# Score products on all 128 array rows in a two-layer hybrid trunk

## The chip, the core and the metric

The kernel runs on one core of a Trainium2 chip. A core has five engines with queues of their own: TensorE (matrix products; PE in the profile, its weight loads PEld), VectorE (DVE), ScalarE (ACT), GpSimd (POOL) and SyncE (SP), which issues the transfers here. The metric is the device time of one execution in microseconds (us); less is better. The time of the kernel before is the median of three runs, 1939.88 us (1935.67 to 1942.19).

## The reference

A trunk of two layers works on 512 latent tokens and 256 context tokens of width 1024, all in float32. Each layer takes a modulated RMS norm, projects it into four groups of heads, joins what the groups return, projects back, and adds; then a gated MLP of width 2816 with a short convolution does the same. The groups are:

- A: four query heads of 64 features on two key heads, with normalised and rotated q and k, softmax over all 768 keys;
- B: a state-space scan in both directions;
- C: as A, but over a window of 128 latent keys to either side and all context keys, with an extra sink logit;
- D: latent attention, four heads whose q and k have 64 features from a low-rank product and 32 rotated ones, 96 together.

Scores are a product over the head's features, 64 in A and C and 96 in D:

```python
s = jnp.einsum('bqkgd,bnkd->bkgqn', q, k).astype(jnp.float32) * scale
p = jax.nn.softmax(s, axis=-1)
return jnp.einsum('bkgqn,bnkd->bqkgd', p.astype(v.dtype), v)
```

Context tokens are queries too in the first layer, and read context keys only; in the second layer there are latent queries alone.

## The kernel before

Features lie on the partitions and tokens along the columns. To keep float32 accuracy, each operand of a product is held as a high part and a low part (`split`, lines 136 to 138: ScalarE rounds the high part, VectorE subtracts; `psplit`, lines 140 to 142, subtracts on GpSimd), and a product is the sum of high x high, low x high and high x low. Every product is issued by `mm` (line 134), so all of TensorE's products carry that line in the profile, and the names of the tiles tell them apart: psi are projections, pss scores, pspt the transposes of the probabilities, psy the values, psq and psk the up-projections of latent attention.

Grouped attention (A and C, `gqa`, line 617) puts a trick on the 128 rows. A query head has 64 features, so one tile `qh` holds the high part of q in one half of its rows (`rh`) and the low part in the other (`rl`; `get_q`, lines 645 to 649). The tile `kh` has the high part of k in both halves, and `kl` the low part in both (`get_kv`, lines 626 to 633; GpSimd writes `kl`). The first product, `qh` with `kh` over 128 rows, sums high x high and low x high at once. The second, line 668, is cut to the 64 rows `rh` and gives high x low. Each of the two is issued for at most 512 columns of keys at a time: a block of 128 queries over 768 keys takes 512 + 256 columns, C's blocks over 640 or 512 keys take 512 + 128 or 512, context queries take 256. C adds its window's mask by a 128-column bf16 product (`cb`).

Latent attention (D, `mla_prologue`, line 1107) has 64 + 32 features in one tile, so it has separate tiles `dqh`, `dql`, `dkh`, `dkl` and three products of 96 rows each (line 1183). `get_pair` (line 1147) makes the tiles of two heads: it projects q (psq), writes rows 0 to 63 by `split`, rows 64 to 95 from the rotated part, projects k (psk) and does the same; the low part of k's rotated rows is subtracted on GpSimd (`psplit`, dkl). Rows 96 to 127 of these tiles aren't written.

A block's way is the same in all three groups (`attention`, line 585): the scores go to one of two PSUM buffers of two banks; VectorE takes the maximum (nm, line 524), ScalarE the exponential with its sum (p, line 531), VectorE the reciprocal, GpSimd scales p (line 538); three blocks later TensorE transposes p, ScalarE and VectorE split it, and TensorE forms the values. Tiles of heads are prepared up to ten blocks ahead (`AHEAD`).

`run` (line 144) traces several streams side by side by weights: A's attention beside C's projections, C's attention beside the projections of D and B, and the scan of B beside the modulation of later stages and latent attention (lines 1217, 1218, 1233). A scheduler of the language then orders the instructions of each engine by these priorities and assigns buffers (41 of the kind `s3`, 16 of `w4`); each engine works off its own queue in order.

Of the kernel before, what the change touches and what calls it, by code (L numbers as in the profile page):

```python
# [17 lines left out]
D = 1024  # L18
SEQ = 512
CTX = 256  # L20
TOK = SEQ + CTX
# [67 lines left out]
def trunk(ctx: ExitStack, tc: tile.TileContext, a, out):  # L89
# [54 lines left out]
    def run(*streams):  # L144
        """Traces streams side by side, each advanced in proportion to its weight."""
        live = [[g, w, 0.0] for g, w in streams]
        while live:
            s = min(live, key=lambda e: e[2])
            try:
                next(s[0])  # L150
                s[2] += 1.0 / s[1]
            except StopIteration:
                live.remove(s)
# [8 lines left out]

# [1 line left out]
    x = []  # L164
# [24 lines left out]

# [1 line left out]
    cact = P1.tile([128, KD, 32], F32, tag="cact", name="cact")  # L191
# [24 lines left out]
    def mod_pool(l, chs):  # L216
        """The same by Pool, features on partitions; the tensor engine sums the partitions."""
        for hc in [2 * ch + c for ch in chs for c in range(2)]:
            accs = s3("macc", F32, (2, 256))
            for q in range(2):  # L220
                wm = w4("wm", (4, 256), F32)
                nc.sync.dma_start(wm, a["wmod"][l, hc, q])
                for g in range(4):
                    first = q == 0 and g == 0
                    tmp = accs if first else s3("mtmp", F32, (2, 256))
                    for t in range(2):
                        pool.tensor_scalar(tmp[:, t], wm[:, g], cact[:, 4 * q + g, t:t + 1], 1.0, op0=ALU.mult, op1=ALU.mult)  # L227
                    if not first:
                        pool.tensor_tensor(accs, accs, tmp, op=ALU.add)
                    yield  # L230
            ps = b1("psm")
            for t in range(2):
                for i in range(2):
                    mm(ps[:, 2 * t + i:2 * t + i + 1], accs[:, t, 128 * i:128 * i + 128], ones[:, 0:1], True, True)
            dve.tensor_tensor(
                mod[l][:, :, 2 * hc:2 * hc + 2], ps[:, 0:4].rearrange("p (t i) -> p t i", i=2),
                par_at(l, "bmod", 2 * hc, 2).unsqueeze(1).to_broadcast([128, 2, 2]), op=ALU.add)
            yield
# [7 lines left out]

# [1 line left out]
    def rstd_steps(ps, n, w, y):  # L248
        v, t = tiny("nv", w), tiny("nt", w)
        dve.tensor_scalar(v, ps[:, :w], 1.0 / n, EPS, op0=ALU.mult, op1=ALU.add)  # L250
        yield
        # a first guess from the exponent's half, then Newton's steps
        dve.tensor_scalar(t.bitcast(I32), v.bitcast(I32), 1, None, op0=ALU.logical_shift_right)
        yield
        dve.tensor_scalar(y.bitcast(I32), t.bitcast(I32), -1.0, float(0x5F3759DF), op0=ALU.mult, op1=ALU.add)
        yield
        for _ in range(3):
            dve.scalar_tensor_tensor(t, y, -0.5, v, op0=ALU.mult, op1=ALU.mult)
            yield
            dve.tensor_tensor(t, t, y, op=ALU.mult)  # L260
            yield
            dve.scalar_tensor_tensor(y, t, 1.5, y, op0=ALU.add, op1=ALU.mult)
            yield
# [7 lines left out]
    def bcast(cols, segs, tiles, heads=1):  # L271
        """PSUM [128, tokens] whose column t is cols[t] (per group of 128 / heads partitions)."""
        for s, ps in zip(segs, tiles):
# [17 lines left out]
    class Norm:  # L291
        """RMS norm of the residual stream, part by part of the tokens; scaled, shifted and split for products."""

# [87 lines left out]
    def first_item(norm, tiles, halfway=None):  # L381
        """The first products after a norm, each of them advanced as the norm's features come."""
        def load():
# [4 lines left out]
        def begin(hls):  # L388
# [6 lines left out]
            def quanta():  # L395
                cuts = (0, KD) if halfway else (0, KD)
                seen = set()
                for k0, k1 in zip(cuts, cuts[1:]):
                    for i, (sl, s) in enumerate(norm.parts):
# [5 lines left out]
                        for k in range(k0, k1):  # L405
                            norm.step(i, k)
                            for n, (hl, (segs, _), pl, pc) in enumerate(zip(hls, tiles, lat, ctx or lat)):
                                if s not in segs:
                                    continue
                                p = pc if s else pl[:, sl]  # L410
                                # the first two products of the context share a bank
                                for j, (wi, hh) in enumerate(((0, norm.hi), (0, norm.lo), (1, norm.hi))):
# [27 lines left out]
    def gemm(items):  # L440
        """Items are (load, begin): begin(load()) gives the quanta of a product and what follows it; the
        steps that follow are traced beside the next products. The next item is loaded with an item's first
        quantum, or a later one."""
        posts = []
# [35 lines left out]

    # ================= token mixers =================
    def mixers(l, norm, halfway, mods):
# [19 lines left out]

# [1 line left out]
        class Half:  # L504
            """256 queries of a head: two blocks of latent queries, or the context's queries."""

# [110 lines left out]
        def gqa(q, k, vt, sinkp, banded, ys):  # L617
            # the banded group keeps its keys in the order lat0 lat1 ctx0 ctx1 lat2 lat3
            kmap = [(0, 256, 0), (512, 256, 256), (256, 256, 512)] if banded else [(0, TOK, 0)]
# [3 lines left out]
            for kv in range(2):  # L623
# [16 lines left out]
                for hh in range(2):  # L640
# [18 lines left out]

                    def sc_mm(ps, q0, c0, w, masks=(), get_kv=get_kv, get_q=get_q, rh=rh):  # L660
                        kh, kl = get_kv()[:2]
                        qh = get_q()
                        qs = slice(q0, q0 + 128)
                        for o in range(0, w, 512):
                            n = min(512, w - o)
                            mm(ps[:, o:o + n], qh[:, qs], kh[:, c0 + o:c0 + o + n], True, False)
                            ms = [m for m in masks if o <= m[1] < o + n]
                            mm(ps[:, o:o + n], qh[rh, qs], kl[rh, c0 + o:c0 + o + n], False, not ms)
                            for i, (mi, mo) in enumerate(ms):
                                mm(ps[:, mo:mo + 128], cb[:, 0, :], cb[:, mi, :], False, i == len(ms) - 1)  # L670
# [38 lines left out]

# [1 line left out]
        qn = tiny("qn", 1)  # L711
# [35 lines left out]

        # V of A and C and dt of B: tokens on partitions
        def v_item(j, box=[]):
# [31 lines left out]

# [1 line left out]
        def c_post(sc, segs, box):  # L783
# [18 lines left out]

# [1 line left out]
        dq, dkv, d_low = [], [], []  # L804
# [53 lines left out]

# [1 line left out]
        zs, xbc = [], []  # L860
# [47 lines left out]

# [1 line left out]
        y_b = []  # L910
# [13 lines left out]
        def scan():  # L924
# [10 lines left out]
            for n in (15, 13, 11, 9, 7, 5, 3):  # L935
# [7 lines left out]
                                     op0=ALU.mult, op1=ALU.mult)  # L943
            # per (direction, chunk, head): running sums, decay of a chunk, weights of its state
            cs, tot, wd, dec, dtd = (tiny(n) for n in ("cs", "tot", "wd", "dec", "dtd"))
# [155 lines left out]

# [1 line left out]
        y_d = []  # L1103
# [3 lines left out]
        def mla_prologue():  # L1107
# [36 lines left out]
            yield  # L1144
            halves = mla_halves
            for pr in range(2):
                def get_pair(pr=pr):
                    qps = up_q(pr)
                    r = []
                    for hh in range(2):  # L1150
                        hd = 2 * pr + hh
                        rh = slice(64 * hh, 64 * hh + 64)
                        qh_, ql_ = s3("dqh", F32R), s3("dql", F32R)
                        for s, p in zip(qsegs, qps):
                            split(qh_[0:64, SEG[s]], ql_[0:64, SEG[s]], p[rh])
# [8 lines left out]
                    for hh in range(2):  # L1164
                        rh = slice(64 * hh, 64 * hh + 64)
                        kh_, kl_ = s3("dkh", F32R), s3("dkl", F32R)
                        for s, p in zip(both, kps):
                            split(kh_[0:64, SEG[s]], kl_[0:64, SEG[s]], p[rh])
# [6 lines left out]
                for hh in range(2):  # L1175
                    hd = 2 * pr + hh

                    def sc_mm(ps, q0, segs, get_pair=get_pair, hh=hh):
                        qh_, ql_, kh_, kl_ = get_pair()[0][hh]
                        qs = slice(q0, q0 + 128)  # L1180
                        for jj, (q_, k_) in enumerate(((qh_, kh_), (ql_, kh_), (qh_, kl_))):
                            for o, sl in segs:
                                mm(ps[:, o:o + sl.stop - sl.start], q_[0:96, qs], k_[0:96, sl], jj == 0, jj == 2)

# [49 lines left out]

# [1 line left out]
        for y in y_d:  # L1236
# [37 lines left out]

    # ================= channel mixer =================
    def ffn(l, norm, nxt, pool_chs):
# [143 lines left out]
    def halfway(k):  # L1420
# [3 lines left out]
        if k == HB:  # L1424
            for _ in chunks:
                pass
            # what is needed later stays behind the modulation
            for t, src in ((con[:, N_CON0:], a["con"][:, N_CON0:]), (cb, a["cb"]), (par[1], a["par"][1])):
# [150 lines left out]
```

## Time and profile before

| | |
|---|---|
| median of three runs | 1939.88 us |
| span of the profiled execution | 1931.3 us |
| TensorE busy | 1847.4 us, 96% |
| VectorE busy | 1109.1 us, 57% |
| ScalarE busy | 782.6 us, 41% |
| GpSimd busy | 517.5 us, 27% |
| mean granted TensorE clock | 0.967 of full speed |

The profile gives no time of its own for the profiled execution beyond its span. Busy means that an instruction of that engine was under way; products overlap one another, so the step from one product's start to the next one's start tells more than their durations.

### The profile page before, as it was taken

How to read it: one execution, taken by the hardware profiler on the slowest of the kernel's cores; microseconds unless marked ns; L12 is line 12 of the kernel's file. 1: busy time of each engine (PE TensorE's matmuls, PEld its weight loads, DVE VectorE, ACT ScalarE, POOL GpSimd, SP SyncE). 2: the span in 40 equal slices, each digit the busy share in tenths (PEclk: the TensorE clock that was granted, in tenths of full speed). 3: DMA queues.
4: the chain of work that ended last, by engine and by line, in shares of the span. 5: the costliest groups of instructions: out<-in, count | busy, mean ns of one | idle time of the engine just before them, and what ended most of it. 6: DMA issues, size and time to landing. Idle time of an engine off the chain costs nothing.

```text
span 1931.3 us, 29356 instructions
## 1 busy us (share of the span) xinstructions
PE 1847.4 (96%) x11552; PEld 1584.6 (82%) x11552; DVE 1109.1 (57%) x2194; ACT 782.6 (41%) x1454; POOL 517.5 (27%) x547
## 2 busy tenths in 40 slices
PE   5999999999999999999999999999998999999997
PEld 3978889668788888888888888888867888888886
DVE  4646466678446545554554464657488475555545
ACT  3455555458334222222222244565448352323222
POOL 0342521436127233322241045251135110000001
PEclk9979899988999999999999998999998999999999
DMA  8101014601322222222222220111822322323221
GB/s 297 55 12 45 22 31 157 230 1 62 113 77 84 75 83 77 78 76 88 70 84 66 71 72 12 33 34 34 306 78 88 99 99 77 120 77 114 83 88 55
DMA packets 50569, 165.20 MB, mean 86 GB/s; under 512 B 5632, under 2 KB 9600, under 8 KB 50304
## 3 DMA queue, kind: packets, MB, share of 16 engines
q1 hardware_dynamic: 50432, 163.33, 24.9%
q8 instruction: 91, 1.49, 0.3%
q14 instruction: 46, 0.38, 0.1%
HBM read 159.12 MB, written 4.19 MB: 85 GB/s over the span
## 4 chain that ended last, share of the span: by engine, by line
PE 86%; DVE 7%; ACT 4%; issue 1%; DMA 1%; POOL 1%; SPq 0%; POOLq 0%; DVEq 0%; ACTq 0%
PE psi L134 41%; PE psd L134 16%; PE pss L134 6%; PE pso L134 6%; PE psy L134 3%; PE psf L134 3%; PE pspt L560 3%; PE psm L134 2%; PE psv L134 2%; PE psn L134 1%; DMA x<-in_xT_dram 1%; DVE ht L357 1%; ACT p L531 1%; DVE wlo L138 1%; PE psq L134 1%
## 5 line engine op out<-in xcount | busy, mean ns | idle before, releaser
L134 PE MATMUL psi<-hhi,whi 128*128 128x256 f32 (+2 forms) x1600 | 492.3, 330 | 4.8 <-DVE fc L1335 2.7
L134 PE MATMUL psi<-hlo,whi 128*128 128x256 f32 (+2 forms) x1600 | 488.7, 328 | 0.0
L134 PE MATMUL psi<-hhi,wlo 128*128 128x256 f32 (+2 forms) x1600 | 487.8, 328 | 0.0
L138 DVE TENSOR_TENSOR wlo<-raw,whi 128x1024 fp32r<-128x1024 f32 (+2 forms) x188 | 241.2, 1283 | 157.1 <-ACT whi L137 111.1
L134 PEld LDWEIGHTS psi<-hhi,whi 128*128 128x128 f32 (+1 forms) x1600 | 288.9, 190 | 32.3 <-DVE fc L1335 2.9
L137 ACT CAST whi<-raw 128x1024 fp32r<-128x1024 f32 (+2 forms) x188 | 195.1, 1039 | 283.8 <-DMA raw<-in_wup_dram 116.2
L134 PEld LDWEIGHTS psi<-hhi,wlo 128*128 128x128 f32 (+1 forms) x1600 | 288.5, 190 | 26.3
L134 PEld LDWEIGHTS psi<-hlo,whi 128*128 128x128 f32 (+1 forms) x1600 | 288.8, 190 | 25.8
L1297 DVE SCALAR_TENSOR_TENSOR x<-psd,mod,x 128x512 f32<-128x512 f32 (+1 forms) x248 | 153.2, 644 | 179.3 <-PE psd L134 178.3
L323 POOL TENSOR_TENSOR sq<-sq,sq 128x256 f32<-128x256 f32 (+1 forms) x45 | 44.9, 999 | 554.3 <-ACT sq L321 534.0
L134 PE MATMUL psd<-ulo,whi 128*128 128x512 f32 (+1 forms) x552 | 167.9, 349 | 0.0
L134 PE MATMUL psd<-uhi,wlo 128*128 128x512 f32 (+1 forms) x552 | 167.3, 348 | 0.0
L134 PE MATMUL psd<-uhi,whi 128*128 128x512 f32 (+1 forms) x552 | 166.2, 348 | 0.0
L538 POOL TENSOR_SCALAR p<-p,sm 128x768 f32<-128x768 f32 (+3 forms) x120 | 98.9, 830 | 187.2 <-DVE sm L536 120.6
L524 DVE TENSOR_REDUCE nm<-pss 128x1 f32<-128x768 f32 (+2 forms) x96 | 85.0, 886 | 66.9 <-PE pss L134 66.3
L531 ACT ACTIVATE p<-pss,nm 128x768 f32<-128x768 f32 (+3 forms) x120 | 93.1, 778 | 60.4 <-DVE nm L524 20.0
L227 POOL TENSOR_SCALAR mtmp<-wm,cact 128x256 f32<-128x256 f32 x112 | 63.7, 584 | 187.9 <-DMA wm<-in_wmod_dram 147.0
L1316 ACT ACTIVATE fc<-psi,par 128x512 f32<-128x512 f32 (+1 forms) x60 | 42.3, 706 | 175.6 <-PE psi L134 175.6
L134 PEld LDWEIGHTS psd<-uhi,whi 128*128 128x128 f32 x552 | 94.3, 189 | 13.5
L134 PEld LDWEIGHTS psd<-uhi,wlo 128*128 128x128 f32 x552 | 93.7, 189 | 14.1
L134 PEld LDWEIGHTS psd<-ulo,whi 128*128 128x128 f32 x552 | 93.3, 188 | 13.5
L560 PE MATMUL pspt<-con,p 128*128 128x128 f32 x528 | 89.1, 294 | 1.4 <-DVE plo L138 0.6
(267 smaller groups left out, 3327.4 us busy)
## 6 DMA issues: line engine op xcount, KB each, us to landing
wm<-in_wmod_dram SPq DMA_DIRECT2D x96, 512.0 KB, 6.5
raw<-in_wup_dram SPq DMA_DIRECT2D x88, 512.0 KB, 3.4
raw<-in_wdn_dram SPq DMA_DIRECT2D x44, 512.0 KB, 3.3
raw<-in_win_dram SPq DMA_DIRECT2D x34, 512.0 KB, 3.6
raw<-in_wout_dram SPq DMA_DIRECT2D x16, 512.0 KB, 3.4
x<-in_xT_dram SPq DMA_DIRECT2D x8, 384.0 KB, 6.6
x<-in_xT_dram SPq DMA_DIRECT2D x8, 256.0 KB, 7.7
xd<-x SPq DMA_DIRECT2D x8, 256.0 KB, 2.0
```

The source lines that it names most:

```text
L134: pe.matmul(out, lhsT, rhs, start=start, stop=stop, **kw)
L137: act.copy(hi, src)
L138: dve.tensor_tensor(lo, src, hi.bitcast(F32), op=ALU.subtract)
L227: pool.tensor_scalar(tmp[:, t], wm[:, g], cact[:, 4 * q + g, t:t + 1], 1.0, op0=ALU.mult, op1=ALU.mult)
L323: eng.tensor_tensor(self.sq[0][:, sl], self.sq[0][:, sl], sq[:, sl], op=ALU.add)
L357: dve.scalar_tensor_tensor(t, x[k][:, sl], self.sct[:, s, k:k + 1], self.ps[:, sl], op0=ALU.mult, op1=ALU.mult)
L524: dve.tensor_reduce(nm, ps[:, :width], axis=AX.X, op=ALU.max, negate=True)
L531: act.activation(p[:, i], v[:, i], AF.Exp, bias=nm[:, i:i + 1], accum_out=sm[:, i:i + 1])
L538: pool.tensor_scalar(p[:, i], p[:, i], sm[:, i:i + 1], 1.0, op0=ALU.mult, op1=ALU.mult)
L560: pe.transpose(pt[:, 128 * (j - j0):128 * (j - j0) + 128], p[:, 0, 128 * (j - t0):128 * (j - t0) + 128], ident)
L1297: dve.scalar_tensor_tensor(x[m][:, sl], p, mod[l][:, s, 40 + m:41 + m], x[m][:, sl], op0=ALU.mult, op1=ALU.add)
L1316: act.activation(c[:, b:e], p, AF.Identity, bias=par_at(l, "fcb", j), scale=par_at(l, "fcw", 3 * j + 1))
```

## The change

The second product of grouped attention takes `qh` and `kl` over all 128 rows (so low x low is added to the sum). The tiles of latent attention get zeros in rows 96 to 127, copied on GpSimd from a block of zeros in the identity matrix, before the other rows are written, and the three products take 128 rows. Some comment lines and docstrings go as well; they issue nothing.

```diff
-                    def sc_mm(ps, q0, c0, w, masks=(), get_kv=get_kv, get_q=get_q, rh=rh):
+                    def sc_mm(ps, q0, c0, w, masks=(), get_kv=get_kv, get_q=get_q):
...
-                            mm(ps[:, o:o + n], qh[rh, qs], kl[rh, c0 + o:c0 + o + n], False, not ms)
+                            mm(ps[:, o:o + n], qh[:, qs], kl[:, c0 + o:c0 + o + n], False, not ms)
...
+            def pad_rows(t, w):
+                pool.tensor_copy(t[96:128, :w].rearrange("p (a b) -> p a b", b=64),
+                                 ident[96:128, 0:64].unsqueeze(1).to_broadcast([32, w // 64, 64]))
+
...
                         qh_, ql_ = s3("dqh", F32R), s3("dql", F32R)
+                        for t in (qh_, ql_):
+                            pad_rows(t, QW)
...
                         kh_, kl_ = s3("dkh", F32R), s3("dkl", F32R)
+                        for t in (kh_, kl_):
+                            pad_rows(t, TOK)
...
-                                mm(ps[:, o:o + sl.stop - sl.start], q_[0:96, qs], k_[0:96, sl], jj == 0, jj == 2)
+                                mm(ps[:, o:o + sl.stop - sl.start], q_[:, qs], k_[:, sl], jj == 0, jj == 2)
```

`QW` is 768 in the first layer and 512 in the second, `TOK` is 768.

## Rows read from the trace of the kernel before

**Rows 1.** The head of the page.
```profile
span 1931.3 us, 29356 instructions
```
**Rows 2.** Windows by stage: stretch, length, busy time (instructions) of PE, PEld, DVE, ACT, POOL, clock, DMA.
```profile
104.00:187.00 83.00, 79.22 (x428) 60.24 (x427) 48.97 (x97) 45.29 (x105) 29.31 (x32) 0.88 0.09 26
206.00:300.00 94.00, 92.71 (x637) 81.08 (x636) 59.90 (x157) 50.40 (x120) 31.11 (x32) 0.93 0.10 29
1195.00:1260.00 65.00, 63.95 (x362) 50.02 (x363) 41.59 (x83) 35.57 (x77) 21.28 (x22) 0.87 0.08 25
1260.00:1345.00 85.00, 83.89 (x628) 74.15 (x627) 53.48 (x137) 49.66 (x115) 36.81 (x38) 1.00 0.11 32
410.00:497.00 87.00, 77.27 (x431) 64.13 (x430) 65.97 (x143) 64.19 (x142) 38.24 (x35) 0.82 0.21 73
1437.00:1497.00 60.00, 50.53 (x314) 42.72 (x312) 50.04 (x111) 47.86 (x110) 30.51 (x27) 0.91 0.20 71
```
**Rows 3.** The chain of waits from 100 to 206 us, by line.
```profile
by line: PE psi L134 35.0%; PE pss L134 25.6%; PE psy L134 13.5%; PE pspt L560 11.1%; DVE nm L524 2.7%; ACT p L531 2.4%; PE pspt L551 1.5%; ACT phi L137 1.4%; ACT phl L137 1.2%; ACT L531 1.2%; issue 1.0%; ACT yt L582 0.7%; DVE nm L518 0.6%;
```
**Rows 4.** The tile pss: second products of grouped attention; duration ns min/median/max, forms.
```profile
L134 PE MATMUL pss<-kl,qh x128: 323/492/793, 104.5 to 1344.3; 64*128 64x512 f32 x64, 64*128 64x256 f32 x48, 64*128 64x128 f32 x16
```
**Rows 5.** Timeline of PE: start us, length us, what; a block of A and the product before it.
```profile
162.35 0.28 PE L134 MATMUL psy<-phi,vhl 128*128 128x256 f32 x1
162.47 0.39 PE L134 MATMUL pss<-kh,qh 128*128 128x512 f32 x1
162.79 0.50 PE L134 MATMUL pss<-kl,qh 64*128 64x512 f32 x1
163.22 0.38 PE L134 MATMUL pss<-kh,qh 128*128 128x256 f32 x1
...
163.84 0.33 PE L134 MATMUL psy<-plo,vhl 128*64 128x256 f32 x1
```
**Rows 6.** Timeline of PE: latent scores (x2 is 512 + 256 keys).
```profile
453.57 0.52 PE L134 MATMUL pss<-dkh,dqh 96*128 96x512 f32 x2
453.92 0.52 PE L134 MATMUL pss<-dkh,dql 96*128 96x512 f32 x2
...
456.22 0.28 PE L134 MATMUL pss<-dkh,dql 96*128 96x256 f32 x1
456.34 0.28 PE L134 MATMUL pss<-dkl,dqh 96*128 96x256 f32 x1
```
**Rows 7.** Timeline of PE: the 128-column pair of a block of C.
```profile
1277.88 0.31 PE L134 MATMUL pss<-kh,qh 128*128 128x128 f32 x1
...
1278.37 0.23 PE L134 MATMUL pss<-cb 128*128 128x128 bf16 x1
```
**Rows 8.** Timeline of PE: a block of A at half clock, and the next one's start.
```profile
110.83 0.80 PE L134 MATMUL pss<-kh,qh 128*128 128x512 f32 x1
...
113.30 0.58 PE L134 MATMUL pss<-kh,qh 128*128 128x256 f32 x1
```
**Rows 9.** Windows, tile pss alone: busy time of PE, PEld, DVE, ACT, then the clock.
```profile
110.10:130.60 20.50, 12.80 (x22) 6.07 (x22) 4.69 (x6) 4.54 (x11) 0.50 0.00 0
1195.50:1212.60 17.10, 11.91 (x21) 5.72 (x20) 4.79 (x5) 4.97 (x10) 0.50 0.00 0
```
**Rows 10.** Timeline of PEld: weight loads of the block in rows 5.
```profile
162.35 0.19 PEld L134 LDWEIGHTS pss<-kh,qh 128*128 128x128 f32 x1
162.79 0.18 PEld L134 LDWEIGHTS pss<-kl,qh 64*128 64x128 f32 x1 [0.24 <-issue]
```
**Rows 11.** Groups on POOL by form: count, busy us, mean ns, idle before.
```profile
L538 POOL TENSOR_SCALAR p<-p,sm 128x768 f32<-128x768 f32 x64 | 58.6, 920 | 81.2 <-DVE sm L536 74.6 <-PE pspt L560 4.6 <-PE pss L134 0.5
L142 POOL TENSOR_TENSOR dkl<-kr,dkh 32x768 fp32r<-32x768 f32 x8 | 14.4, 1809 | 22.3 <-ACT dkh L141 10.2 <-PE psk L134 6.9 <-issue 5.1
```
**Rows 12.** Timeline of POOL: the first kl and the first dkl.
```profile
91.38 3.76 POOL L632 TENSOR_TENSOR kl<-ak,kh 64x768 fp32r<-64x768 f32 x2 [18.20 <-ACT kh L630]
...
422.63 3.60 POOL L142 TENSOR_TENSOR dkl<-kr,dkh 32x768 fp32r<-32x768 f32 x2 [6.94 <-PE psk L134]
```

## The prediction

> **What bounds the kernel now.** I read the page first: the profiled execution spans 1931.3 us [rows 1]. The page gives this execution no other time; the median of the three timed runs is 1939.88 us, so 8.6 us lie around the span, and I leave them as they are. Then the table of windows, cut at the stages in which grouped attention runs (104 to 187 and 206 to 300 us in layer 0, 1195 to 1260 and 1260 to 1345 us in layer 1) and latent attention (410 to 497, 1437 to 1497 us) [rows 2]. In the four grouped stretches TensorE is busy for all but 3.8, 1.3, 1.05 and 1.1 us, while VectorE fills 59%, 64%, 64% and 63%. The chain of waits says the same of the first stage: psi, pss, psy and pspt, all on TensorE, make up 85% of it [rows 3]. So there a shorter TensorE stream is a shorter stage. The latent stretches differ: TensorE is idle 9.7 of 87 and 9.5 of 60 us, VectorE is 76% and 83% busy.
>
> **Change 1: the second grouped product over 128 rows.** Nothing is added or removed: 128 products keep their columns, 64 of 512, 48 of 256 and 16 of 128, and lose their cut at 64 rows [rows 4]. A 64-row product always stands between 128-row ones, so I price the pair, from the start of the first product to the start of what follows the second. In a clean place at the full clock the pair over 512 keys takes 163.22 - 162.47 = 0.75 us and the pair over 256 keys 163.84 - 163.22 = 0.62 us [rows 5]. For what equal heights cost, the latent products are the nearest rows: three of 96 rows follow one another, each with another pair of operands and its own weight load. One over 768 keys takes 453.92 - 453.57 = 0.35 us and one over 256 takes 0.12 us, so one over 512 takes 0.23 us [rows 6]. The gain of a pair is therefore 0.75 - 0.46 = 0.29 us at 512 and 0.62 - 0.24 = 0.38 us at 256. At 128 columns the pair takes 0.49 us [rows 7]; I allow the price of 256 columns, 0.12 us, for each half, which leaves at least 0.25 us. Sum: 64 x 0.29 = 18.6, 48 x 0.38 = 18.2, 16 x 0.25 = 4.0, together 40.8 us.
>
> Some pairs run at half clock. A query block over 768 keys (a 512 and a 256 pair) takes 113.30 - 110.83 = 2.47 us there [rows 8]; four equal-height products would take at most twice their full-clock 0.70 us, so the gain is 1.07 instead of 0.67 us. The two long half-clock stretches (granted clock 0.50, 1.2 of 2.4 GHz) hold 22 and 21 such products, about 10.75 blocks [rows 9]: 10.75 x 0.40 = 4.3 us more. TensorE's saving is 45.1 us.
>
> What is late next? The second product now also waits for the other half of kl. That costs nothing: both halves for the first heads are written by 95.1 us, nine before the first score [rows 12]; later heads are prepared up to ten blocks ahead. But ScalarE and VectorE must still give each block its maximum, exponential and splits. The first stage would shrink from 83 by 4.6 + 9.1 + 2.2 = 15.9 us (by the code four heads of four blocks, so 16 pairs of 512 and 16 of 256, and 8 of 256 for the context, and half of the 4.3) to 67.1 us, with VectorE at 49.0/67.1 = 73%; its fellow in layer 1 from 65 by 12.9 to 52.1 us, VectorE 80%. That is how full VectorE is in the latent stretches, where TensorE idles 11% and 16%. At these shares the stages would wait 7.4 and 8.3 us instead of 3.8 and 1.05, giving back 3.6 + 7.3 = 10.9 us. As projection products are traced between these blocks and fill part of such waits, I take 4 us, between 0 and 10.9. The other two stages carry more projection work; I take nothing there.
>
> A rule of the Trainium skill speaks against this part. In this trace the weight load of the first score product starts at 162.35, beside the 128-row product that starts at 162.35 and 0.12 us ahead of its own at 162.47, while that of the 64-row product starts at 162.79 together with its product, after 0.24 us in which no weights were loaded [rows 5, 10]. "TensorE: Matmul & The Clock Gate", Part 3 (packing small matmuls), holds that weight loads overlap with running matmuls only when the row groups differ. By that rule equal heights win no overlap and the sum would be 0; the load at 162.35 overlaps a product of its own height, so the trace disagrees.
>
> **Change 2: latent products from 96 to 128 rows.** A 96-row product over 256 keys takes 0.12 us [rows 6], and a 128-row product of 256 columns takes the same 162.47 - 162.35 = 0.12 us [rows 5]. What is left between them is under the 0.01 us that these rows resolve, at 216 latent products 2 us to either side; I take 0.
>
> **Change 3: the zeros.** Each layer has 2 pairs x 2 heads x 4 tiles = 16 new GpSimd copies of 32 rows by 768 (512 for q in layer 1), 32 in all. Before shows no GpSimd copy. The nearest rows are the one-input scaling of 768 columns, 0.92 us, and the two-input subtraction on 32 rows, 1.81 us [rows 11]. By shape a copy is the former: at most 32 x 0.92 = 29.4 us of GpSimd, 58 us at the upper end. They need only a free buffer, so they can run early; GpSimd is idle 6.94 us before the first dkl [rows 12], against 8 x 0.92 = 7.4 us for a pair's eight. Behind them in GpSimd's queue stand dkl (the third score product waits for it) and the scaling of p (the transposes wait for that); the first score product now waits for the zeros too. With cover the price is 0; all exposed, 14.7 us a layer. I take 1.5 us a layer, 3 us, near the low end since TensorE still has the second pair's projections to do meanwhile. No DMA is added or moved; what sync issues after these stages moves earlier with them.
>
> Sum: 45.1 - 4 - 3 = 38 us; 1931.3 - 38 = 1893 of span, 1902 us as timed.
>
> **Rivals.** (a) The clock. The first long half-clock stretch begins 110.1 - 104.5 = 5.6 us after the first 64-row product, the other also lies at the start of a stage of A [rows 4, 9]. If denser products keep it at 2.4 GHz, the 37.6 us there, less 10.75 x 1.07 = 11.5 already saved, shrink to half: 13 us more, 1889; with no waits and hidden zeros, 1882. Against it: the first blocks still wait for ScalarE. (b) ScalarE and VectorE become the limit everywhere: the windowed stages too wait 11% of their 163 us instead of 2.4, giving back 15.5, with the 10.9 above: 45.1 - 26.4 - 3 = 16 us, 1924. For it: VectorE would reach 70%; against: projection products there fill waits. (c) The pair's price is no matter of height but of the weight load that isn't ahead of its product, or of the bank in which the two accumulate: TensorE saves nothing, and the time is 1940, with the zeros 1943. Against it: latent products accumulate in one bank too, each with a load of its own, without the price [rows 6]. The rule from "TensorE: Matmul & The Clock Gate" would lead here. (d) Slower: the zeros hold up GpSimd's queue before latent attention. At 1.81 us each and wholly on the path they cost 58 us: 45.1 - 4 - 58 is a loss of 17, 1957. It decides from 41/32 = 1.3 us exposed per copy. Against it: the idle time in rows 12.
>
> **How the numbers follow.** The forecast (gain 28 to 45 us) 0.58, (a) 0.17, (b) 0.16, (c) 0.04, (d) 0.03; 0.02 for a new order of work at the stages' ends that costs a little more or less than it gives. The range reaches from (a) without waits, 1882, less part of what the second stage loses at its mean clock of 0.93 (0.07 x 94 = 6.6 us [rows 2]), so 1878, up to (b), 1924. A change under 0.3% (6 us) can't be told from none here. Forecast, (a) and (b) are faster: 0.92 with part of the rest; same 0.04, slower 0.04.
>
> **What would show it.** Right: no 64-row pss form; blocks of 768 keys take 0.70 us; TensorE's busy time falls by about 45 us, nearly all in the four stages; 32 short copies on GpSimd. Wrong: pairs still at 0.62 to 0.75 us (c); unchanged stage lengths with new waits for ACT p or POOL p (b); dkl landing several us later than its psk, and longer latent stretches (d); half clock absent after the first blocks (a).

## The result and the profile after

The changed kernel takes 1911.87 us (median of four runs, 1908.92 to 1914.4) against 1937.78 us for the kernel before on the same chip: a ratio of 0.9882, with a 95% interval of 0.9846 to 0.9918, some 23 us less. The forecast was 1902 us, 38 us less. One run of one kernel below (first pair's zeros early) took 2028.27 us at a granted clock of 0.83, and that kernel's numbers leave it out. The profiled execution went from 1931.3 to 1907.1 us of span, 24.2 us less. The head of the page and its table of busy time:

```profile
span 1907.1 us, 29376 instructions
PE 1802.8 (95%) x11552; PEld 1568.0 (82%) x11552; DVE 1112.1 (58%) x2194; ACT 783.3 (41%) x1454; POOL 543.7 (29%) x579
```

TensorE is busy 44.6 us less and GpSimd 26.2 us more, with 32 more instructions. The windows of the same stretches as in [rows 2]: the four of grouped attention run from the same places of the program, the two latent ones from the same distance after the scan's first product to the same distance from the products that follow the attention. Columns as there:

```profile
101.60:171.00 69.40, 62.07 (x431) 54.83 (x431) 48.13 (x98) 45.53 (x106) 29.84 (x32) 0.95 0.10 31
189.50:274.50 85.00, 81.88 (x635) 76.65 (x634) 60.79 (x157) 49.79 (x119) 31.11 (x32) 0.96 0.10 32
1177.70:1228.50 50.80, 47.73 (x362) 43.91 (x362) 40.02 (x81) 34.84 (x76) 21.24 (x22) 1.00 0.10 32
1228.50:1310.70 82.20, 79.44 (x631) 73.91 (x629) 54.25 (x138) 49.53 (x114) 36.88 (x38) 0.98 0.11 33
383.90:479.40 95.50, 76.73 (x450) 61.48 (x447) 69.59 (x146) 64.43 (x145) 48.28 (x46) 0.89 0.19 66
1402.50:1472.70 70.20, 58.75 (x319) 46.33 (x317) 51.29 (x115) 49.04 (x110) 33.77 (x31) 0.85 0.18 61
```

This table holds the whole result. Grouped attention shrank by 13.6, 9.0, 14.2 and 2.8 us, together 39.6 us. Latent attention grew by 8.5 and 10.2 us, together 18.7 us. The difference, 20.9 us, and 2.4 us less ahead of the first score are nearly the whole 24.2 us.

What a block of A costs now, from the timeline of TensorE (start, length, what); it answers to [rows 5]:

```profile
150.96 0.50 PE L134 MATMUL pss<-kh,qh 128*128 128x512 f32 x1
151.29 0.39 PE L134 MATMUL pss<-kl,qh 128*128 128x512 f32 x1
151.53 0.28 PE L134 MATMUL pss<-kh,qh 128*128 128x256 f32 x1
151.64 0.28 PE L134 MATMUL pss<-kl,qh 128*128 128x256 f32 x1
```

No product of 64 rows is left. The steps 151.53 - 151.29 = 0.24 us and 151.64 - 151.53 = 0.11 us are those of the latent products in [rows 6]. Over all full-clock blocks of 768 keys that run without a pause inside, from the first product's start to the start of what follows, the median, worked out from those starts, is 0.78 us of 22 blocks after and 1.46 of 18 before, 0.67 us less before rounding, as forecast. The 0.70 us of the forecast is what the fastest of them take.

The long half-clock stretches have mostly gone. Windows of the tile pss (busy time of PE, PEld, DVE, ACT, then the clock), the places of [rows 9] and the one low stretch that is left in the first stage:

```profile
106.20:113.00 6.80, 5.49 (x16) 4.05 (x16) 2.88 (x4) 3.69 (x10) 0.50 0.00 0
1178.00:1195.10 17.10, 5.70 (x26) 4.06 (x24) 6.61 (x7) 6.89 (x15) 1.00 0.01 1
```

The 20.5 us at 1.2 GHz are now 6.8 us, and the 17.1 us of layer 1 run at 2.4 GHz.

The zeros on GpSimd, grouped by tile and form (count, busy us, mean ns, idle before), and the low part of k, which stands behind them in its queue:

```profile
L1148 POOL CAST dkl<-con 32x768 fp32r<-32x768 f32 x8 | 7.8, 973 | 0.0
L1148 POOL CAST dql<-con 32x512 fp32r<-32x512 f32 x4 | 2.4, 612 | 0.0
L142 POOL TENSOR_TENSOR dkl<-kr,dkh 32x768 fp32r<-32x768 f32 x8 | 14.4, 1807 | 3.6 <-ACT dkh L141 3.3
```

All 32 add up to 27.5 us, just under the 29.4 us that the prediction worked out for them. What they did can be read on VectorE in layer 0, on the last step of the rotation of q (line 501: the sum of two parts, of which GpSimd makes one):

```profile
389.84 1.32 DVE L499 TENSOR_TENSOR qr<-qrw,con 128x512 f32<-128x512 f32 x1
...
392.43 0.23 DVE L138 TENSOR_TENSOR vd<-psv,vd 128x64 fp32r<-128x64 f32 x1 [1.01 <-ACT vd L137]
395.19 0.68 DVE L138 TENSOR_TENSOR dql<-psq,dqh 64x512 fp32r<-64x512 f32 x1 [2.54 <-ACT dqh L137]
...
405.91 1.48 DVE L138 TENSOR_TENSOR dkl<-psk,dkh 64x256 fp32r<-64x256 f32 x3
407.31 0.68 DVE L501 TENSOR_TENSOR qr<-qr,rsh 128x512 f32<-128x512 f32 x1
```
```profile
390.69 1.41 POOL L500 TENSOR_TENSOR rsh<-rsh,con 128x512 f32<-128x512 f32 x1
```

GpSimd's part was there at 390.69 + 1.41 = 392.10 us, VectorE's own at 391.16. VectorE then stood idle for 2.54 us, and the sum ran only at 407.31: it stands behind the splits of both pairs of heads in VectorE's queue. In the kernel before, it ran within 0.2 us of GpSimd's part. So this is the order of the queue, not a late operand. ScalarE's high part of q waits for that sum, and TensorE for that; its longest waits in the latent stretch of layer 0 (total us, times, longest):

```profile
PE pss L134 <- ACT p L531: 5.4, 7, 1.8
PE pss L134 <- ACT dqh L1164: 4.3, 1, 4.3
```

In the kernel before the second of these did not occur, and the first took 3.6 us. There, in layer 0, the first pair's first scores stood ahead of the second pair's projections on TensorE, which filled the wait for the first exponentials; now they stand behind them, and nothing fills it. TensorE in layer 0, before and then after:

```profile
423.32 1.06 PE L134 MATMUL pss<-dkh,dqh 96*128 96x512 f32 x2
424.42 0.77 PE L134 MATMUL psq<-chi,wq 128*128 128x512 f32 x1
```
```profile
404.44 0.28 PE L134 MATMUL psk<-chi,wk 128*128 128x256 f32 x1
409.06 1.62 PE L134 MATMUL pss<-dkh,dqh 128*128 128x512 f32 x4 [4.33 <-ACT dqh L1164]
```

The first score comes 11.8 us later after the scan's start than before in layer 0, 8.8 us in layer 1. In layer 1 the order changed less: there the second pair's q products and half of its k products stood ahead of the first score in the kernel before too. And the two layers lose in different ways. From the scan's first product to the first product after attention, TensorE's idle time rose from 17.5 to 27.9 us in layer 0, and its busy time fell by 2.0; in layer 1 idle time rose only from 12.7 to 15.0 us and busy time by 7.9, at a mean granted clock of 0.91 instead of 0.94.

### The profile page after: what moved, and what is told of

Same layout as the page of the kernel before. It is cut to its first block, busy times and chain, and to the rows that moved or that the text cites. A ratio compares the mean times of both kernels' runs of the same rounds, so it can differ in the third digit from the quotient of the medians.

```text
span 1907.1 us, 29376 instructions
## 1 busy us (share of the span) xinstructions
PE 1802.8 (95%) x11552; PEld 1568.0 (82%) x11552; DVE 1112.1 (58%) x2194; ACT 783.3 (41%) x1454; POOL 543.7 (29%) x579
## 4 chain that ended last, share of the span: by engine, by line
PE 83%; DVE 9%; ACT 4%; issue 2%; DMA 1%; POOL 1%; SPq 0%; POOLq 0%; DVEq 0%; ACTq 0%
PE psi L134 41%; PE psd L134 16%; PE pso L134 5%; PE psf L134 3%; PE pss L134 3%; PE psy L134 3%; PE psm L134 2%; PE pspt L560 2%; PE psv L134 2%; ACT p L531 1%; DVE nm L524 1%; PE psq L134 1%; PE psn L134 1%; DVE ht L357 1%; DMA x<-in_xT_dram 1%
## 5 line engine op out<-in xcount | busy, mean ns | idle before, releaser
L134 PEld LDWEIGHTS psi<-hhi,wlo 128*128 128x128 f32 (+1 forms) x1600 | 288.3, 190 | 26.2
L560 PE MATMUL pspt<-con,p 128*128 128x128 f32 x528 | 82.4, 277 | 4.3 <-POOL p L538 2.0
```

The costliest lines, as they stand in the source:

```text
L134: pe.matmul(out, lhsT, rhs, start=start, stop=stop, **kw)
L560: pe.transpose(pt[:, 128 * (j - j0):128 * (j - j0) + 128], p[:, 0, 128 * (j - t0):128 * (j - t0) + 128], ident)
```

## The experiments

Each was timed in three rounds beside the kernel before; the table has the ratio to it and the change of the two latent stretches in the profiled execution, from the scan's first product to the first product after attention (before: 149.9 and 116.7 us).

| kernel | median us | ratio (95%) | latent stretches |
|---|---|---|---|
| after | 1911.87 | 0.9882 (0.9846 to 0.9918) | +8.5, +10.3 |
| grouped change alone | 1895.85 | 0.9796 (0.9764 to 0.9829) | +1.9, +5.9 |
| latent change alone | 1948.74 | 1.0073 (1.0045 to 1.0101) | +9.4, +10.3 |
| zeros unread | 1915.10 | 0.9893 (0.9868 to 0.9917) | +11.7, +11.0 |
| zeros of 64 columns, unread | 1899.95 | 0.9822 (0.9792 to 0.9851) | +4.9, +6.3 |
| second pair's zeros, unread | 1911.97 | 0.9891 (0.9858 to 0.9923) | +11.4, +7.4 |
| first pair's zeros, unread | 1912.05 | 0.9883 (0.9857 to 0.9910) | +10.4, +8.9 |
| first pair's zeros early | 1908.61 | 0.9861 (0.9829 to 0.9892) | +12.3, +2.5 |
| zeros last | 1910.99 | 0.9879 (0.9851 to 0.9907) | +8.6, +12.8 |
| zeros on ScalarE | 1909.81 | 0.9863 (0.9835 to 0.9890) | +11.7, +9.0 |
| rotation on VectorE, zeros | 1918.29 | 0.9914 (0.9887 to 0.9941) | +12.3, +13.2 |
| rotation on VectorE, no zeros | 1897.17 | 0.9812 (0.9777 to 0.9847) | +1.9, +6.8 |
| before, heights grouped | 1920.31 | 0.9924 (0.9898 to 0.9950) | +1.3, +5.3 |

**The two halves.** The grouped change alone is the kernel before with line 668 unsliced; the latent change alone is the kernel after with it sliced again:

```diff
-mm(ps[:, o:o + n], qh[rh, qs], kl[rh, c0 + o:c0 + o + n], False, not ms)
+mm(ps[:, o:o + n], qh[:, qs], kl[:, c0 + o:c0 + o + n], False, not ms)
```

> The grouped part alone: second product over 128 rows, latent products left at 96 rows, no zeros. The four grouped stretches gained about 41 us in the trace of the changed kernel and the two latent stretches lost 18.8. If all of that loss belongs to the zeros, this kernel is 41 us faster than before, some 1896 us, and first score of latent attention comes 78 us (layer 0) and 65 us (layer 1) after the scan's start, as before. Rival, the latent stretch suffers because the grouped stage ends earlier (buffers, weights of the modulation): the loss stays and the time is about 1912 us. A third, 96 rows cost something beside 128-row neighbours: then latent products of 768 keys take over 0.35 us here and 0.35 us in the changed kernel.

> The zeros and the 128-row latent products alone; grouped attention's second product stays at 64 rows. If the zeros cost what the changed kernel's latent stretches lost, 8.5 and 10.3 us, this is 19 us slower than before, about 1957 us. If the loss came from the earlier end of the grouped stages, it is within 3 us of before.

The first is 1895.85 us, faster than both kernels; the second is slower than before. So the latent change costs 0.73% (14 us, from 9 to 20 by the interval) by itself and 0.86% (17 us, give or take some 9) on top of the grouped one, and the grouped change is worth 2.04% (39 us) alone. The latent change alone came out between its two expectations (19 us slower, or within 3), nearer to the theory of the zeros. The two latent stretches of the grouped change alone:

```profile
384.86:473.70 88.84, 78.75 (x440) 64.63 (x436) 67.49 (x146) 64.51 (x144) 38.27 (x35) 0.82 0.21 71
1396.79:1462.71 65.92, 54.06 (x324) 45.88 (x323) 55.00 (x122) 48.86 (x115) 30.72 (x27) 0.87 0.19 65
```

They grew by 1.8 and 5.9 us without a single zero. So on top of the grouped change the zeros account for about 11 of the 18.7 us in the profiled executions; the timed runs say 14 to 17. The two growths don't simply add up: the latent change alone, without the shorter grouped stages, lengthens the two stretches by 19.7 us (table). The growth without zeros seems to go with the shorter grouped stages, not with 128 rows in them: the last row of the table keeps its 64-row products, is shortened otherwise, and shows 1.3 and 5.3 us.

**Height or copies.** Zeros written as in the kernel after, but the latent products read 96 rows:

```diff
-mm(ps[:, o:o + sl.stop - sl.start], q_[:, qs], k_[:, sl], jj == 0, jj == 2)
+mm(ps[:, o:o + sl.stop - sl.start], q_[0:96, qs], k_[0:96, sl], jj == 0, jj == 2)
```

> The kernel after, with the zeros written as there but the latent products cut to 96 rows again, so that nothing reads them. Theory that the copies themselves cost the time (GpSimd is taken, VectorE beside it slowed, the order of the streams changed by them): as after, 1908 to 1914. Theory that the 128-row products cost it (they wait for the zeros, or their greater height is not free): as the kernel with the grouped change alone, 1894 to 1899.

The whole loss stays, as the first theory has it. Neither the height of the products nor their reading of the zeros costs anything that can be seen; the copies do.

**How long the copies are.** The same, and each copy writes 64 columns:

```diff
 def pad_rows(t, w):
+    w = 64
     pool.tensor_copy(t[96:128, :w]...
```

> As the kernel with unread zeros (1915), but each copy writes 64 columns instead of 768 or 512: the same 32 instructions at the same places, each taking its buffer as early, GpSimd hardly busy with them (some 0.1 to 0.2 us each). Theory of GpSimd's time (6.6 us of copies a pair stand in its queue, in the real run and in the order drawn up beforehand, ahead of the rotation's sine product or of the scores): the loss goes, 1894 to 1900 as with the grouped change alone, and the rotation's last sum lies within 4 us of where it lay before. Theory of buffers or of the mere count (a tile that gets zeros is taken earlier, and one more writer has to be waited for): as with full zeros, 1908 to 1916.

```profile
L1149 POOL CAST dql<-con 32x64 fp32r<-32x64 f32 x8 | 3.7, 458 | 5.1 <-PE psyb L134 3.2 <-DVE yb L1056 1.9
L1149 POOL CAST dkh<-con 32x64 fp32r<-32x64 f32 x8 | 1.9, 236 | 0.1
```

All 32 still take 9.9 us, more than expected, and by the ratios 14 of the 19 us between the full zeros and none come back: the length of the copies is most of what costs, not their number. The second half of the expectation failed. The rotation's sum lies 7.2 us later than before in both layers, and in layer 0 VectorE again has an idle stretch ahead of it while both parts are ready (GpSimd's since 391.84 us):

```profile
397.76 0.68 DVE L138 TENSOR_TENSOR dql<-psq,dqh 64x512 fp32r<-64x512 f32 x1 [3.88 <-ACT dqh L137]
398.37 0.67 DVE L501 TENSOR_TENSOR qr<-qr,rsh 128x512 f32<-128x512 f32 x1
```

So the place of the sum in the queue moves with the length of copies on another engine: behind one split here, behind the splits of both pairs with full copies.

**Which copies.** The same with full copies, but for one pair of heads only (`if pr == 1 else ()`, and `pr == 0`):

```diff
-for t in (qh_, ql_):
+for t in (qh_, ql_) if pr == 1 else ():
     pad_rows(t, QW)
```

> As the kernel with unread zeros (1915), but only the second pair of latent heads gets them: 16 copies instead of 32. Theory of the first chain (the loss arises because the first pair's eight copies stand between its projection and the first score, with no other latent scores yet to fill TensorE): nearly no loss, 1895 to 1902. Theory of the sum (each copy costs the same wherever it stands): half of the loss, 1903 to 1907.

> As the kernel with unread zeros (1915), but only the first pair of latent heads gets them: the other 16 copies. Theory of the first chain: nearly the whole loss, 1908 to 1915. Theory of the sum: half of it, 1903 to 1907.

Either half costs as much as both, so both theories fall: the loss is neither a sum over copies nor one place in the first pair's chain. With the first pair's zeros the first score is 15.3 and 11.2 us late. With the second pair's it is in time (+2.8 and +0.9 us), and the loss comes later, in layer 0 mostly as a lower clock:

```profile
384.06:482.47 98.41, 86.02 (x439) 69.32 (x436) 69.51 (x146) 64.75 (x144) 46.03 (x43) 0.77 0.18 64
```

TensorE is busy 7.3 us longer there than with the grouped change alone (78.75), for the same products, at a mean granted clock of 0.77 instead of 0.82. Over the whole kernel the four runs have a granted clock of 0.966 to 0.969, and 0.969 to 0.976 in a kernel without zeros that was timed beside it (below: rotation on VectorE, no zeros), so this is hardly a chance of one execution. What brings it about is open.

**Where the copies stand.** First: the eight tiles of the first pair are taken and zeroed at the head of the latent stage. Second: all zeros are written at the end of `get_pair`. Third: `act.copy` in place of `pool.tensor_copy`.

```diff
+def four(pr, hh):   # tiles and zeros of a head, once
...
+for hh in range(2):
+    four(0, hh)
```

> The kernel after, with the eight tiles of the first pair of latent heads taken and their zeros written at the head of the latent stage instead of at the first use; the second pair's zeros stay where they are. Theory of place (GpSimd's copies beside VectorE's work on the pair are what makes the first scores late): half of the copies move off that moment, the latent stretches return 4 to 8 us each, 1897 to 1905. Theory of order (the first scores are traced as depending on more work, and go behind the second pair's projections in TensorE's queue): no more than 3 us a layer, 1907 to 1912. Theory of buffers (eight tiles held earlier make the scan and the other streams wait for a free buffer): 1912 or more.

```diff
-for t in (qh_, ql_):
-    pad_rows(t, QW)
...
+for four in r:
+    for t in four[:2]:
+        pad_rows(t, QW)
+    for t in four[2:]:
+        pad_rows(t, TOK)
```

> The changed kernel with the zeros written in the program behind everything else of a pair, not ahead of it; count and engine are the same. Theory of the order: the rotation's last sum is no longer put off, so the loss shrinks; the first score still needs its zeros, so I expect 4 to 12 us of the 18.8 back, 1900 to 1908 us. Theory of the queue: dkl now goes ahead of the zeros, but the first score waits for zeros that come later; no gain or a further loss, 1912 us or more.

```diff
-pool.tensor_copy(t[96:128, :w]...
+act.copy(t[96:128, :w]...
```

> The kernel after, with the zeros copied by ScalarE instead of GpSimd: the same 32 copies at the same place, and GpSimd has as little to do as in the kernel before. Theory that GpSimd's copies beside VectorE (each slows the other) and what GpSimd's queue puts off cause the loss: most of the 18.8 us of the latent stretches comes back less 16 short copies a layer on ScalarE, of which perhaps half are exposed: 1896 to 1904. Theory that the wait of the first score for more writes causes it, whichever engine writes: 1910 to 1916. Rival that ScalarE is the scarcer engine there (it makes the high parts and the exponentials): 1915 to 1925.

None recovers the loss: all three lie within 4 us of the kernel after. The first is where its theory of order put it (1907 to 1912), the second falls between its two ranges, the third just under that of a wait for more writes, whichever engine writes (1910 to 1916); but what is late differs. Traced early, the first pair's copies of layer 0 ran from 373.3 us, but the second pair's followed from 385.8 to 395.2 us, ahead of the rotation's part on GpSimd, and the sum came 25.4 us later than before; in layer 1 the same edit left only 2.5 us of loss. Written last, the sum is in time in layer 0 (+1.3 us; +8.0 in layer 1), and the first scores stand behind most of the second pair's projections anyway (+9.5). On ScalarE, GpSimd is free and the sum early in layer 0 (-0.9 us; +2.7 in layer 1), but ScalarE's queue is full of copies, of which these are some:

```profile
396.90 0.83 ACT L1148 CAST dqh<-con 32x768 fp32r<-32x768 f32 x1
397.63 0.82 ACT L1148 CAST dql<-con 32x768 fp32r<-32x768 f32 x1
...
402.74 0.58 ACT L137 CAST dqh<-psq 64x512 fp32r<-64x512 f32 x1
```

The split at 402.74 had its projection from 391 to 394 us, and TensorE waited 8 us for ScalarE's dkh ahead of the first score.

**The narrow theory: only the rotation's sum.** GpSimd's part of the rotation moved to VectorE, beside the zeros and without them:

```diff
-pool.tensor_tensor(sh[rows, LAT], sh[rows, LAT], sin[rows], op=ALU.mult)
+eng.tensor_tensor(sh[rows, LAT], sh[rows, LAT], sin[rows], op=ALU.mult)
...
-rope(qr, qrw, C("cosM"), C("sinM"), SWAP8)
+rope(qr, qrw, C("cosM"), C("sinM"), SWAP8, eng=dve)
```

> The changed kernel with one edit: the sine product in the rotation of latent q is issued on VectorE instead of GpSimd, so that the final sum of the rotation waits for nothing on GpSimd. Zeros and 128 rows stay. Theory of the order: the zeros' price is that the scheduler, reckoning with a busy GpSimd, put the rotation's last sum (VectorE) behind the splits of both pairs of heads, so that first scores came 12 and 9 us late; here the sum comes early and most of the 18.8 us return: about 1896 us, first score 77 to 81 us after the scan's start in layer 0. Theory of the queue: the 16 copies on GpSimd themselves hold up dkl and the scaling of p; they are all still there, and the time stays at 1909 to 1914 us.

> The grouped change alone (no zeros, latent products of 96 rows, 1896), with the rotation's sine product of latent q on VectorE as in the experiment that moved it beside the zeros (1918). It shows what that move costs by itself: 0.7 us more on VectorE per layer and two engine changes fewer, so 1893 to 1899 if VectorE has room; if VectorE is the scarce engine before the first score, 1900 or more, and then the run with the zeros said little of the zeros.

The move costs nothing without zeros (1897.17 against 1895.85). With them the sum came early in layer 0 (+2.5 us; +9.3 in layer 1) and the loss was no smaller, 1918 us where the two theories gave 1896 and 1909 to 1914. So the put-off sum is the form that the loss takes in the kernel after, not its only form. In this run there is another: VectorE is busy 1122.2 us against 1113.5 without the zeros, as some of its work ran beside GpSimd's (last section). In the kernel after this hardly plays a part: VectorE is busy 1112.1 us there, and 1111.9 with the grouped change alone.

**The price of a change of height.** The kernel before, with a block's products in the order full, full, 64, 64 rows:

```diff
     mm(ps[:, o:o + n], qh[:, qs], kh[:, c0 + o:c0 + o + n], True, False)
+for o in range(0, w, 512):
+    n = min(512, w - o)
...
     mm(ps[:, o:o + n], qh[rh, qs], kl[rh, c0 + o:c0 + o + n], False, not ms)
```

> The kernel before with the grouped products of a block put in another order: both products of all rows (512, then 256 keys), then both products of 64 rows, instead of full, half, full, half. Same products, same loads, same sum; a block of two chunks changes height twice instead of four times. Theory of the height (each change between 64 and 128 rows costs time, the equal-height order nothing): the 48 blocks with a 256 (or 128) second chunk lose two of four changes, about 0.3 us each block and somewhat more at half clock: 13 to 17 us less, about 1920. Rival (the price belongs to each 64-row product by itself, or to its weight load, wherever it stands): as before, 1934 to 1938.

```profile
152.48 0.51 PE L134 MATMUL pss<-kh,qh 128*128 128x512 f32 x2
152.93 0.61 PE L134 MATMUL pss<-kl,qh 64*128 64x512 f32 x2
153.47 0.33 PE L134 MATMUL psy<-plo,vhl 128*64 128x256 f32 x1
```

0.76% or 15 us less (10 to 20 by the interval), as the theory of the height says: this block takes 153.47 - 152.48 = 0.99 us, between 1.37 with four changes [rows 5] and 0.70 with none. Two 64-row products in a row pay once, so the price belongs to the change and not to the product. The weight loads show it from both sides (PEld):

```profile
152.92 0.29 PEld L134 LDWEIGHTS pss<-kl,qh 64*128 64x128 f32 x2 [0.25 <-issue]
153.46 0.13 PEld L134 LDWEIGHTS psy<-plo,vhl 128*64 128x64 f32 x1 [0.24 <-issue]
```

And in the kernel after, where all heights are equal (its products are those shown from 150.96 on):

```profile
151.07 0.19 PEld L134 LDWEIGHTS pss<-kl,qh 128*128 128x128 f32 x1
151.30 0.19 PEld L134 LDWEIGHTS pss<-kh,qh 128*128 128x128 f32 x1
```

The load after each change of height starts only with its own product; the loads within one height run ahead, here by 151.29 - 151.07 = 0.22 and 151.53 - 151.30 = 0.23 us.

## Why the gain fell short of the forecast

The time is 10 us above the forecast; the gain, forecast at 38 us, is 23 us by the ratio and 24.2 us of span, so 14 to 15 us short. That is what the zeros cost beyond their 3 us.

- **Grouped pairs, 45.1 us less 4.** Right in the mechanism and in the price of a pair. The four stages shrank by 39.6 us against 41.1, and the grouped change alone measured 39 us. That the sum came so near is partly luck, as two terms missed in opposite directions: TensorE's busy time in the four stages fell by 48.7 us, 3.6 more than 45.1, and 9.1 us were given back, 5 more than 4. Nor does the 44.6 us by which TensorE's busy time fell over the whole kernel confirm the 45.1: it is 48.7 less in these stages, 5.9 more from the scan's start to the end of attention, both layers together, and 1.9 less elsewhere.
- **The 4 us given back.** Too small. TensorE's idle time in the four stages rose from 3.8, 1.3, 1.05 and 1.1 us to 7.3, 3.1, 3.1 and 2.8. For the first stage the working had 7.4 us of wait, which came; for its fellow in layer 1 it had 8.3, and 3.1 came; the two windowed stages, taken at nothing, gave back 3.5. The reduction to 4 us for fillers was not borne out.
- **Rival (a)** came true in part: the 37.6 us at 1.2 GHz became 6.8, but busy time fell by only 3.6 us more than the forecast, not by 13. **Rival (b)** did in part: waits grew, but only by a third of what it gave. **Rival (c)** fell: the saving came, and the two products of a pair still accumulate in one bank. The load that isn't ahead of its product is there, but it goes with the change of height. By the rule of the Trainium skill that went with it ("TensorE: Matmul & The Clock Gate", Part 3), equal heights lose the overlap; the loads above run ahead within one height and stop at a change of height, so the trace differs.
- **96 to 128 rows, 0.** Right: with zeros unread the time is the same.
- **The zeros, "1.5 us a layer, 3 us".** This step failed, and it is the one that cost the gain. The price is 14 us alone and 17 us on top of the grouped change; their size (27.5 us of GpSimd) was right, the share that shows was taken as a tenth and is more than half. The argument was that GpSimd is idle ahead of the first dkl [rows 12] and that TensorE has the second pair's projections to do meanwhile. GpSimd's idle time was real, and the first dkl came even earlier than before (72.9 against 77.2 us after the scan's first product). But with the copies the order of the queues was another, and in layer 0 the projections that were to cover the wait ran ahead of the scores instead of beside their softmax.
- **Rival (d)** had the right place, GpSimd's copies before latent attention, and the wrong way: the copies hardly held up GpSimd's queue (its part of the rotation in layer 0 was ready to start at 389.94 us and started at 390.69), and at 17 us the loss stayed under the saving.

What is shown: the cost comes from the copies, grows with their length and not with their reading, and in layer 0 of the kernel after it arrives as an order of VectorE's and TensorE's queues in which ready work waits. What stays open: by what rule the order is drawn, so why half of the copies cost as much as all, and why layer 1, where the sum ran some 10 us after its two parts were there, loses in TensorE's busy time at a lower clock (0.85 against 0.91 in the windows) and hardly in its idle time (11.5 against 9.5 us; from the scan's start to the end of attention, 15.0 us in the kernel after and with the grouped change alone). Nor was it settled why the latent stretches grew by 1.8 and 5.9 us without zeros.

## What to carry to other kernels

Products of unequal height in one stream cost 0.29 to 0.38 us here for each way in and out, at the full clock, so make them equal where the extra rows are there already, or put equal ones together. Where the extra rows must first be written, price the writing by what it does to the order of the queues ahead of the first dependent product, not by the idle time of the engine that writes. When each part of a change can be run alone, run it: one half of this change was worth 39 us, and the other took 14 to 17 us back.

## What the runs showed of the hardware

VectorE and GpSimd can slow each other down; it depends on what VectorE does. Two timelines of the run with the second pair's zeros, GpSimd and then VectorE:

```profile
403.18 1.57 POOL L1148 CAST dqh<-con 32x768 fp32r<-32x768 f32 x1
404.69 1.55 POOL L1148 CAST dql<-con 32x768 fp32r<-32x768 f32 x1
406.19 0.82 POOL L1148 CAST dqh<-con 32x768 fp32r<-32x768 f32 x1
```
```profile
403.11 0.95 DVE L1165 TENSOR_TENSOR dql<-qr,dqh 32x768 fp32r<-32x768 f32 x1 [0.16 <-ACT dqh L1164]
404.09 0.43 DVE L138 TENSOR_TENSOR dkl<-psk,dkh 64x256 fp32r<-64x256 f32 x1
404.54 1.01 DVE L1165 TENSOR_TENSOR dql<-qr,dqh 32x768 fp32r<-32x768 f32 x1
```

The copy takes 1.55 us beside VectorE's subtractions of line 1165, which read two tiles in SBUF, and 0.82 us where VectorE stands idle from 405.6 us on. On ScalarE the copies of this size took 0.82 to 0.83 us on average. The Trainium skill ("GPSIMD Engine Reference", Specifications) states such a contention for VectorE operations with two SBUF inputs; the rows agree, and give its size. In the other direction the sum of line 501 takes 0.69 us in the kernel before and 2.18 us where it ran beside GpSimd's dkl, in the run with the rotation on VectorE:

```profile
L501 DVE TENSOR_TENSOR qr<-qr,rsh x1: 2181/2181/2181, 392.1 to 392.1; 128x512 f32<-128x512 f32 x1
L1165 DVE TENSOR_TENSOR dql<-qr,dqh x4: 1393/1484/2368, 395.2 to 400.7; 32x768 fp32r<-32x768 f32 x4
```

The four subtractions of the second row took 0.95 us each in the same kernel without zeros, where nothing of GpSimd's ran beside them; here they ran beside its copies and its dkl. So work on an otherwise idle GpSimd need not be free for VectorE.
